# A delta-rule encoder step: faded queries and keys made in the projection stage and kept in DRAM, decay rows from one transposition

## Chip, core and metric

One NeuronCore of a Trainium2 chip. The metric is the device time of one execution in microseconds (us), lower is better. All data are float32; most matrix products are made of three passes with a value split into a rounded high part and a rest.

## What is computed

The reference is one inference step of a two-layer encoder for 2048 prompt tokens and 32 sample tokens with a model width of 1024. Only its first layer is touched here, the gated delta rule with 8 heads of 128:

```
qkv = silu(causal_conv(x @ w_in))          # q, k, v, 4 taps
q = l2norm(q) * 128**-0.5 ; k = l2norm(k)
gcum = cumsum of the log decay within a block of tokens
qdec = q * exp(gcum) ; kdec = k * exp(gcum_last - gcum)
v_new = u - (T (beta k exp(gcum))) S        # what the state recalls for a key
o = qdec S + (q k^T * decay) v_new
S = S * exp(gcum_last) + kdec^T v_new
```

The factor exp(gcum) on queries and keys is called the fade here. Behind the layer stand an output projection with a layer norm, then a sliding-window attention layer; neither is changed.

## The kernel before

**Layout.** Tokens lie along the free axis in the first stage: 2080 columns, in 5 blocks of 416 (TB). In the delta stage they are cut into 17 chunks: 16 of 128 prompt tokens, and one of the 32 sample tokens. Between the two stages q, k, v and the gate z go through DRAM scratch, stored as (chunk, channel, head, token).

**First stage (P1).** 24 rows of 128 output channels (8 heads of q, of k, of v), then 8 of the gate. For each row i:

- `block` (L300), five times: 24 matmuls of 416 columns into one PSUM bank (`project`, L75 to L83), then ScalarE (ACT) copies the bank into the row's buffer R (L305). `ps` (L145) deals the banks out in turn, two from one pool (L108) and four from another (L112); R has two buffers.
- `conv` (L198) for the row just finished, while TensorE (PE) makes the next: ACT writes y = R times the first tap (L206); VectorE (DVE) adds three taps (L209); ACT makes tanh into th (L213); DVE makes silu (L215); SyncE (SP) stores y to q, k or v (L218; the piece of the 32 sample tokens at L220, on ACT's queue before row 15). For q and k ACT squares y into th (L223), DVE transposes th into R (L225) and reduces it to parts (L226). th has one buffer, and in rows 6 to 14 the splitting of the output weights (L1091, `split_out_weights`) borrows it.
- `norms` (L456) after the eighth row of q and of k.

`gates` (L373) is called after rows 0 and 1. It computes the decays and ends in a loop of 17 turns (L422 to L430): PE transposes an 8-column slice of gcum for one chunk, DVE copies it to g_row (one buffer), ACT makes its exponential, and ACT's queue stores both, to `gcum` and `grow` in DRAM.

**What sets the order.** Up to row 15 a scheduler orders each engine's queue. From row 16 on `ordered` (L232) writes the order out by hand for all five engines: each turn of its loop starts row i on PE and `conv(i - 1)`, and between the five blocks advances `conv` (2, 2, 1, 1, 0 steps) and `decays` (L262), which loads `gcum` rows broadcast to all partitions, adds a mask (DVE, L284), makes exponentials (ACT, L288) and stores the decay matrices E (SP, L289; the next load is L277). A weight fetch (L48) is issued in the third block. Engines work their queues in order, so an instruction that waits holds up all that stand behind it on its engine.

**Delta stage (Delta, L605).** `ORDER` is a list of steps with a chunk offset each; for PE, DVE and ACT it is the order of the queues, SP is left to the scheduler. Steps that matter here: `Lk`, `Lq`, `Lgb` load k, q and the decay row of a chunk (`grow`, broadcast to 128 partitions); `G` (L695) are the products of keys; `tk` turns k (L809); `gq` (L822) multiplies queries and keys; `fk`, `fq0`, `fq1` are the fades, products on DVE in place (L832): k after `tk`, q after `gq`; `ks` (L837) recalls with the faded k; `os` (L861) reads the state with the faded q. `L`, `T1` to `T3` and `SPR1` are the transposition and the chain on DVE and GpSimd (POOL) that invert a triangular matrix and end in tcp (L746), which PE needs for y1p (L765). Up to chunk turn 11 the matmuls of the gate rows left over (`GA`) are placed between; after it, not. The output projection of finished chunks is put in at the end.

## Time and profile before

| | |
|---|---|
| median of 3 runs | 2135.41 us (2134.36 to 2135.69) |
| the profiled execution | 2134.49 us, of which its span is 2132.4 us |
| granted clock of PE | 0.996 |
| DMA | 307.25 MB, mean 144 GB/s |

The profile is of one execution. A row of the time line gives start, duration, engine, line of the kernel, operation, output<-inputs, shapes, how many instructions were merged, and in brackets the idle time before it and what ended it. SPq and ACTq are the queues that issue DMAs. In waits, the three numbers are us in total, times, and the longest. Busy time of PE is a modelled time, since matmuls are pipelined.

### The profile page before, as it was taken

The numbers are of one execution on the slowest core, as the hardware profiler recorded it, in microseconds if no ns is written. First come the engines' busy times: TensorE is split into PE (matmuls) and PEld (weight loads), VectorE is DVE, ScalarE is ACT, GpSimd is POOL, SyncE is SP. The second block draws the span as 40 slices with busy tenths as digits, with TensorE's granted clock in tenths as the row PEclk, the third lists the DMA queues.
The fourth block names the chain that finished last, engine by engine and source line by source line (L and its number), as shares of the span: only waits on it lengthen the run. The fifth ranks groups of instructions, "written<-read, shape, count | busy, mean of one in ns | idle before, by whom it ended". The sixth has DMA issues, their size and how long they took to land.

```text
span 2132.4 us, 37157 instructions
## 1 busy us (share of the span) xinstructions
PE 2098.1 (98%) x14062; PEld 1933.3 (91%) x14062; DVE 1305.4 (61%) x2449; ACT 894.0 (42%) x2215; POOL 830.3 (39%) x1179
## 2 busy tenths in 40 slices
PE   8999999999999999999999999999999998999998
PEld 6999999999999999999988888999999996777775
DVE  3676676666557688778977886224543223566665
ACT  4444434446522466667752212312111234455552
POOL 1422222222222277777840201236443113466665
PEclk9999999999999999999999999999999999999999
DMA  5222333256674544446856764556221257534321
GB/s 204 70 62 88 104 110 103 83 145 191 195 215 143 175 158 161 159 150 201 267 178 201 225 211 121 158 174 221 77 78 69 78 132 250 154 99 115 104 71 65
DMA packets 263634, 307.25 MB, mean 144 GB/s; under 512 B 71408, under 2 KB 194608, under 8 KB 263184
## 3 DMA queue, kind: packets, MB, share of 16 engines
q1 hardware_dynamic: 252208, 281.40, 42.3%
q10 hardware_dynamic: 11248, 23.48, 3.4%
q8 instruction: 111, 1.82, 0.4%
q14 instruction: 67, 0.55, 0.1%
HBM read 188.58 MB, written 116.60 MB: 143 GB/s over the span
## 4 chain that ended last, share of the span: by engine, by line
PE 92%; DVE 3%; DMA 3%; ACT 1%; issue 1%; POOL 0%; SPq 0%; ACTq 0%; POOLq 0%; DVEq 0%
PE ps L79 17%; PE ps L81 17%; PE ps L80 17%; PE po L1139 3%; PE ot L1137 3%; PE po L1137 3%; PE po L1138 3%; PE ot L1139 3%; PE ot L1138 3%; PE S L1689 2%; PE ot L1722 2%; PE tr L1704 2%; PE g L695 2%; PE ks L837 1%; PE gq L822 1%; PE op L861 1%
## 5 line engine op out<-in xcount | busy, mean ns | idle before, releaser
L79 PE MATMUL ps<-act_hi,w_hi 128*128 128x416 f32 x1936 | 683.1, 354 | 0.4 <-ACT w_hi L55 0.4
L81 PE MATMUL ps<-act_hi,w_lo 128*128 128x416 f32 x1936 | 681.3, 352 | 1.2 <-POOL w_lo L56 1.2
L80 PE MATMUL ps<-act_lo,w_hi 128*128 128x416 f32 x1936 | 678.1, 350 | 0.4 <-DVE act_lo L71 0.4
L79 PEld LDWEIGHTS ps<-act_hi,w_hi 128*128 128x128 f32 x1936 | 364.1, 188 | 5.5 <-ACT w_hi L55 0.8
L80 PEld LDWEIGHTS ps<-act_lo,w_hi 128*128 128x128 f32 x1936 | 363.7, 188 | 4.8 <-DVE act_lo L71 0.8
L81 PEld LDWEIGHTS ps<-act_hi,w_lo 128*128 128x128 f32 x1936 | 363.4, 188 | 5.0 <-POOL w_lo L56 1.7
L56 POOL TENSOR_TENSOR w_lo<-w_raw,w_hi 128x1024 fp32r<-128x1024 f32 x44 | 117.0, 2658 | 471.6 <-ACT w_hi L55 435.7
L209 DVE SCALAR_TENSOR_TENSOR y<-R,convw,y 128x2083 f32<-128x2083 f32 x72 | 183.0, 2543 | 62.7 <-ACT y L206 47.0
L1528 POOL TENSOR_TENSOR P<-e,sm 128x384 f32<-128x384 f32 (+2 forms) x128 | 101.2, 813 | 182.0 <-DVE sm L1518 176.0
L729 POOL TENSOR_TENSOR tm<-L,Tt 128x60 f32<-128x60 f32 (+19 forms) x365 | 126.1, 345 | 98.1 <-issue 40.0
L731 POOL TENSOR_TENSOR Tt<-Tt,tm 128x60 f32<-128x60 f32 (+19 forms) x365 | 143.4, 393 | 28.6
L1514 ACT ACTIVATE e<-S,nm 128x193 f32<-128x193 f32 (+2 forms) x260 | 104.8, 416 | 95.7 <-DVE nm L1509 58.1
L1137 PE MATMUL ot<-wo,g_hi 128*128 128x512 f32 x256 | 104.6, 409 | 6.2 <-DMA wo<-s_wob 6.2
L305 ACT COPY R<-ps 128x416 f32<-128x416 f32 (+1 forms) x144 | 60.3, 442 | 108.3 <-PE ps L81 95.6
L1137 PE MATMUL po<-wo_hi,g_hi 128*128 128x512 f32 x256 | 103.4, 404 | 0.0
L1336 POOL TENSOR_TENSOR rs<-rs,sin 128x416 f32<-128x416 f32 x50 | 70.7, 1414 | 79.2 <-DVE rs L1335 73.1
L1139 PE MATMUL ot<-wo,g_lo 128*128 128x512 f32 x256 | 101.2, 395 | 0.0
L1138 PE MATMUL ot<-wo,g_hi 128*128 128x512 f32 x256 | 101.1, 395 | 0.0
L1139 PE MATMUL po<-wo_hi,g_lo 128*128 128x512 f32 x256 | 100.2, 391 | 0.5 <-DVE g_lo L1180 0.5
L1138 PE MATMUL po<-wo_lo,g_hi 128*128 128x512 f32 x256 | 99.9, 390 | 0.0
L1421 DVE SCALAR_TENSOR_TENSOR za<-zs,za 128x416 f32<-128x416 f32 x40 | 31.7, 797 | 111.0 <-ACT za L1420 110.6
L55 ACT CAST w_hi<-w_raw 128x1024 fp32r<-128x1024 f32 x46 | 48.4, 1052 | 92.2 <-PE ps L80 73.7
(299 smaller groups left out, 3950.3 us busy)
## 6 DMA issues: line engine op xcount, KB each, us to landing
w_raw<-in_w_in SPq DMA_DIRECT2D x40, 512.0 KB
w_raw<-in_b_w_in SPq DMA_DIRECT2D x18, 512.0 KB
k<-s_k SPq DMA_DIRECT2D x17, 512.0 KB
E<-s_E SPq DMA_DIRECT2D x17, 512.0 KB
s_bz<-za SPq DMA_DIRECT2D x40, 208.0 KB
s_bq<-ra SPq DMA_DIRECT2D x40, 208.0 KB
s_q<-y SPq DMA_DIRECT2D x8, 1024.0 KB
s_wo<-wo_parts SPq DMA_DIRECT2D x16, 512.0 KB
```

The source lines that it names most:

```text
L56: sub.tensor_tensor(out=lo[:], in0=raw[:], in1=hi[:], op=ALU.subtract)
L79: nc.tensor.matmul(ps, hi[:, k, :], xh[:, k, :], start=(k == 0), stop=False)
L80: nc.tensor.matmul(ps, hi[:, k, :], xl[:, k, :], start=False, stop=False)
L81: nc.tensor.matmul(ps, lo[:, k, :], xh[:, k, :], start=False, stop=(k == KC - 1))
L209: nc.vector.scalar_tensor_tensor(out=y[:], in0=R[:, j:j + W], scalar=self.convw[:, i, j:j + 1], in1=y[:], op0=ALU.mult, op1=ALU.add)
L729: P.tensor_tensor(out=tm[:n, i0 - k:, :w], in0=L[:n, i0:, j:j + 1].to_broadcast(sh), in1=Tt[:n, j:j + 1, :w].to_broadcast(sh), op=ALU.mult)
L731: P.tensor_tensor(out=Tt[:n, i0:, :w], in0=Tt[:n, i0:, :w], in1=tm[:n, i0 - k:, :w], op=ALU.subtract)
L1137: nc.tensor.matmul(ps[:n], ghi[:, k, :n], hi, start=a, stop=False)
L1138: nc.tensor.matmul(ps[:n], ghi[:, k, :n], lo, start=False, stop=False)
L1139: nc.tensor.matmul(ps[:n], glo[:, k, :n], hi, start=False, stop=z)
L1514: self.nc.scalar.activation(x.e[:, h, u, :x.n], x.S[:, h, u, :], AF.Exp, bias=x.nm[:, h, u:u + 1], scale=1.0, accum_out=x.sm[:, h, u:u + 1])
L1528: self.nc.gpsimd.tensor_tensor(out=x.P[:, u, :nj * 128].rearrange("r (j h k) -> r j h k", h=2, k=64), in0=x.e[:, :, u, :n].rearrange("r h ...
```

## The change

- **Faded q and k in the first stage.** In rows 2 to 15, after the third tap, SP loads the head's decay row from `grow` into R, broadcast to 128 partitions (`decay_row`). After the squares DVE multiplies y by it into R (`fade`), and SP stores R to new scratch tensors `qf` (rows 2 to 7) or `kf` (rows 8 to 15). The transposition for the norms now goes to y and not to R. The norms of q move from row 7 into row 8.
- **Heads 0 and 1 of q** pass before the decays exist. `fade_again` loads their q back from DRAM into a y buffer and the decay row into th, at the end of the turns i = 19 and 21 of `ordered`, and multiplies and stores them at the start of turns 20 and 22.
- **Delta stage.** The steps `fk`, `fq0`, `fq1` and the load `Lgb` go; `Lkf`, `Lqf0`, `Lqf1` load kf and qf (kf in the one buffer that gb had). q has two half buffers and qf two, where q had five. `ks` reads kf, `os` reads qf. The rest of ORDER keeps its sequence.
- **Decay rows.** Two transpositions in place of 17: one of the sample chunk's 8 columns, one of all 128 columns of the other chunks. Each is copied to g_row, and its exponential made and stored as before.

```diff
@@ -208,6 +208,8 @@
             yield
             nc.vector.scalar_tensor_tensor(out=y[:], in0=R[:, j:j + W], scalar=self.convw[:, i, j:j + 1], in1=y[:],
                                            op0=ALU.mult, op1=ALU.add)
+        if 2 <= i < 16:
+            self.decay_row(h, R)
         yield
         th = one.tile([128, NT + 3], F32, tag="th", name="th")
         nc.scalar.activation(th[:], y[:], AF.Tanh, scale=0.5)
@@ -222,21 +224,58 @@
             return
         nc.scalar.activation(th[:, 0:NP], y[:, 0:NP], AF.Square)
         nc.scalar.activation(th[:, NP:NT], y[:, NP + 3:NP + 3 + NS], AF.Square)
-        nc.vector.transpose(R[:, 0:NT], th[:, 0:NT])
-        nc.vector.tensor_reduce(out=parts[:, h, :], in_=R[:, 0:NT].rearrange("p (c j) -> p c j", j=32),
+        if i == 8:
+            norms(nc, self.G, parts, self.sel, 0, one, self.pt)
+        sq = R
+        if i >= 2:
+            self.fade(kind, h, R, y, R)
+            sq = y
+        nc.vector.transpose(sq[:, 0:NT], th[:, 0:NT])
+        nc.vector.tensor_reduce(out=parts[:, h, :], in_=sq[:, 0:NT].rearrange("p (c j) -> p c j", j=32),
                                 axis=AX.X, op=ALU.add)
         yield
-        if h == 7:
-            norms(nc, self.G, parts, self.sel, kind, one, self.pt)
+        if i == 15:
+            norms(nc, self.G, parts, self.sel, 1, one, self.pt)
+
+    PIECES = (slice(NP + 3, NP + 3 + NS), slice(0, NP))
+
+    def decay_row(self, h, g):
+
+        nc, src = self.nc, self.T["grow"]
+        nc.sync.dma_start(g[:, self.PIECES[0]], src[NTT - 1, h, 0:NS].partition_broadcast(128))
+        nc.sync.dma_start(g[:, 0:NP].rearrange("p (t k) -> p t k", k=128),
+                          src[0:NTT - 1, h, :].partition_broadcast(128))
+
+    def fade(self, kind, h, g, y, out):
+
+        nc, dst = self.nc, self.T[("qf", "kf")[kind]]
+        for s in self.PIECES:
+            nc.vector.tensor_tensor(out=out[:, s], in0=y[:, s], in1=g[:, s], op=ALU.mult)
+        nc.sync.dma_start(dst[NTT - 1, :, h, 0:NS], out[:, self.PIECES[0]])
+        nc.sync.dma_start(dst[0:NTT - 1, :, h, :].rearrange("t p k -> p t k"),
+                          out[:, 0:NP].rearrange("p (t k) -> p t k", k=128))
+
+    def fade_again(self, h):
+
+        q = self.big.tile([128, NT + 3], F32, tag="y", name="y")
+        g = self.one.tile([128, NT + 3], F32, tag="th", name="gb")
+        src = self.T["q"]
+        self.nc.sync.dma_start(q[:, self.PIECES[0]], src[NTT - 1, :, h, 0:NS])
+        self.nc.sync.dma_start(q[:, 0:NP].rearrange("p (t k) -> p t k", k=128),
+                               src[0:NTT - 1, :, h, :].rearrange("t p k -> p t k"))
+        self.decay_row(h, g)
+        yield
+        self.fade(0, h, g, q, q)
 
     def ordered(self, R, parts):
 
         nc, I = self.nc, self.I
         w = split_weights(nc, self.wp, I["w_in"][self.FREE + 1], nc.gpsimd)
         raw = fetch_weights(nc, self.wp, I["w_in"][self.FREE + 2])
-        matrices = None
+        matrices, again = None, iter(())
         for i in range(self.FREE + 1, 24):
             c = self.conv(i - 1, R, parts)
+            drain(again)
             nxt = self.row(i)
             following = split_fetched(nc, self.wp, raw, nc.gpsimd)
             next(c)
@@ -252,6 +291,9 @@
                     matrices = self.decays()
                     next(matrices)
                 self.block(nxt, w, b)
+            if i in (self.FREE + 4, self.FREE + 6):
+                again = self.fade_again((i - self.FREE - 4) // 2)
+                next(again)
             last = c
             R, w = nxt, following
         self.room = self.one, ("parts", "gtmp")
@@ -419,15 +461,15 @@
     nc.scalar.activation(G["ekd"][:, 0:NTT - 1, :], gl[:, 0:NTT - 1, :], AF.Exp)
     nc.scalar.activation(G["ekd"][:32, NTT - 1, :], gl[:32, NTT - 1, :], AF.Exp)
     V.tensor_scalar(out=G["ngc"][:], in0=gc, scalar1=-1.0, scalar2=None, op0=ALU.mult)
-    for t in range(NTT):
-        n = min(128, NT - t * 128)
+    for a, z, n in ((n0, n0 + H, NS), (0, n0, 128)):
+        m = z - a
         tp = pt.tile([128, 512], F32, tag="tp", name="tp")
-        nc.tensor.transpose(tp[:H, :n], gc[:n, t, :], G["ident"][:n, :n])
-        row = one.tile([H, 2, 128], F32, tag="g_row", name="g_row", bufs=1)
-        V.tensor_copy(row[:, 0, :n], tp[:H, :n])
-        nc.scalar.activation(row[:, 1, :n], tp[:H, :n], AF.Exp)
-        nc.scalar.dma_start(T["gcum"][t, :, :n], row[:, 0, :n])
-        nc.scalar.dma_start(T["grow"][t, :, :n], row[:, 1, :n])
+        nc.tensor.transpose(tp[:m, :n], gcf[:n, a:z], G["ident"][:n, :n])
+        row = one.tile([128, 2, 128], F32, tag="g_row", name="g_row", bufs=1)
+        V.tensor_copy(row[:m, 0, :n], tp[:m, :n])
+        nc.scalar.activation(row[:m, 1, :n], tp[:m, :n], AF.Exp)
+        for c, name in enumerate(("gcum", "grow")):
+            nc.scalar.dma_start(T[name].rearrange("t h k -> (t h) k")[a:z, :n], row[:m, c, :n])
 
 
 def add_log(nc, out, x, one, n, w):
...
@@ -656,14 +697,13 @@
         nc, T, n, ti = self.nc, self.T, ch.n, ch.ti
         own = ch.pool is not None and name not in "zE"
         w = n if own else 128
-        if name in ("gb", "k"):
+        if name in ("kf", "k"):
             if own:
                 t = ch.pool.tile([128, 8, w], F32, tag="c" + name, name=name, bufs=1)
             else:
-                t = self.four.tile([128, 8, w], F32, tag=name, name=name, bufs=1 if name == "gb" else self.BUFS)
+                t = self.four.tile([128, 8, w], F32, tag=name, name=name, bufs=1 if name == "kf" else self.BUFS)
             ch.__dict__[name] = t
-            src = T["grow"][ti, :, :n].partition_broadcast(128) if name == "gb" else T["k"][ti, :, :, :n]
-            nc.sync.dma_start(t[:, :, :n], src)
+            nc.sync.dma_start(t[:, :, :n], T[name][ti, :, :, :n])
         elif name == "E":
             ch.E = self.two.tile([128, 8, 128], F32, tag="E", name="E")
             nc.sync.dma_start(ch.E[:n, :, :n], T["E"][ti, :n, :, :n])
@@ -671,8 +711,8 @@
             for q in halves:
                 if own:
                     t = ch.pool.tile([128, 4, w], F32, tag=f"c{name}{q}", name=name, bufs=1)[:]
-                elif name == "q":
-                    t = self.four.tile([128, 4, w], F32, tag="q", name="q", bufs=5)[:]
+                elif name in ("q", "qf"):
+                    t = self.four.tile([128, 4, w], F32, tag=name, name=name, bufs=2)[:]
                 else:
                     t = self.sml.tile([128, 4, w], F32, tag="vz", name=name, bufs=3)[:]
                 ch.__dict__.setdefault(name, {})[q] = t
@@ -827,10 +867,6 @@
         self.nc.vector.tensor_tensor(out=at[:n, :, :n], in0=g[:n, :, :n], in1=ch.E[:n, self.heads(q), :n], op=ALU.mult)
         ch.__dict__.setdefault("at", {})[q] = at
 
-    def fade(self, ch, x, hs):
-        x = x[:, :, :ch.n]
-        self.nc.vector.tensor_tensor(out=x, in0=x, in1=ch.gb[:, hs, :ch.n], op=ALU.mult)
-
     def products(self, ch, pool, name, q, lhs, rhs, n):
         ps = self.bank(pool, ch, f"{name}{q}")
         for j in range(4):
@@ -838,7 +874,7 @@
 
     def recall(self, ch, q):
         n, S = ch.n, ch.S[q]
-        self.products(ch, self.pc, "ks", q, lambda j: ch.k[:, q * 4 + j, :n], lambda j: S[:, j, :], n)
+        self.products(ch, self.pc, "ks", q, lambda j: ch.kf[:, q * 4 + j, :n], lambda j: S[:, j, :], n)
 
     def errors(self, ch, q):
         n, ks, vn = ch.n, ch.__dict__.pop(f"ks{q}"), ch.vn[q]
@@ -858,7 +894,7 @@
         n = ch.n
         op = self.bank(self.pd, ch, f"op{q}")
         for j in range(4):
-            self.nc.tensor.matmul(op[:n, j, :], ch.q[q][:, j, :n], ch.S[q][:, j, :], start=(j == 0), stop=False,
+            self.nc.tensor.matmul(op[:n, j, :], ch.qf[q][:, j, :n], ch.S[q][:, j, :], start=(j == 0), stop=False,
                                   skip_group_check=True)
 
     def seen_inside(self, ch, q):
...
@@ -942,13 +978,12 @@
                    "z": self.gated, "st": self.store}
             for name, f in two.items():
                 S[f"{name}{q}"] = lambda c, f=f, q=q: f(c, q)
-            for name in "qvz":
+            for name in ("q", "qf", "v", "z"):
                 S[f"L{name}{q}"] = lambda c, name=name, q=q: self.load(c, name, (q,))
             S[f"tk{q}"] = lambda c, q=q: self.turn(c, c.k[:, self.heads(q)], f"ktr{q}")
             S[f"tv{q}"] = lambda c, q=q: self.turn(c, c.v[q], f"vtr{q}")
             S[f"kd{q}"] = lambda c, q=q: self.scaled(c, q, "ktr", "kd", "ekd")
             S[f"vn{q}"] = lambda c, q=q: self.scaled(c, q, "vtr", "vn", "hn")
-            S[f"fq{q}"] = lambda c, q=q: self.fade(c, c.q[q], self.heads(q))
         return S
 
     def save(self, ch):
...
@@ -1046,7 +1081,7 @@
             tmp.k = own.k
             tmps.append(tmp)
         yield
-        for name in ("gb", "q", "v"):
+        for name in ("kf", "q", "qf", "v"):
             self.load(chunks[0], name)
         for ch, tmp in zip(chunks, tmps):
             self.load(tmp, "E")
@@ -2162,6 +2197,8 @@
     "q": (NTT, 128, 8, 128),
     "k": (NTT, 128, 8, 128),
     "v": (NTT, 128, 8, 128),
+    "qf": (NTT, 128, 8, 128),
+    "kf": (NTT, 128, 8, 128),
     "z": (NTT, 128, 8, 128),
     "wo": (2, KC, 128, D),
     "wob": (2, KC, 128, D),
```

19 lines of the change are left out of this document (9 added, 10 removed).

## The prediction

> **What bounds the kernel now.** I read the page first: the busy times, then the stretches of time in which an engine could matter, then what TensorE waited for.
>
> ```profile
> PE 2098.1 (98%) x14062; PEld 1933.3 (91%) x14062; DVE 1305.4 (61%) x2449; ACT 894.0 (42%) x2215; POOL 830.3 (39%) x1179
> ```
>
> TensorE (PE) is busy for 2098.1 of 2132.4 us. The change takes work from VectorE (DVE), which is busy 61%, so it can win only where PE waits for DVE. The view of stretches says where that is; its columns are the stretch, its length, then busy time with instruction counts of PE, PEld, DVE, ACT and POOL, the clock, the DMA share and GB/s.
>
> ```profile
> 491.30:513.80 22.50, 22.50 (x121) 22.35 (x121) 13.51 (x10) 13.89 (x33) 5.28 (x5) 1.00 0.65 210
> 829.35:854.51 25.16, 25.16 (x274) 24.20 (x272) 20.95 (x50) 16.98 (x52) 17.55 (x49) 1.00 0.48 157
> 1000.61:1022.16 21.55, 20.75 (x250) 19.80 (x248) 20.66 (x54) 15.22 (x50) 16.81 (x43) 1.00 0.86 281
> 1022.16:1043.69 21.53, 20.49 (x250) 19.84 (x249) 19.58 (x52) 15.81 (x52) 17.66 (x47) 1.00 0.82 275
> 1043.69:1064.64 20.95, 20.39 (x248) 19.78 (x249) 18.68 (x51) 14.62 (x49) 16.37 (x46) 1.00 0.78 266
> 1064.64:1085.50 20.86, 20.09 (x236) 19.10 (x234) 18.32 (x51) 15.21 (x47) 16.98 (x47) 1.00 0.72 233
> ```
>
> The first row is one row of 120 matmuls in the projection stage, 22.50 us, PE never idle. The second is one chunk of the delta stage with the gate's matmuls between: PE never idle either, and DVE at 20.95 of 25.16 costs nothing. The last four are the chunks after the gates are done: here PE idles 0.80, 1.04, 0.56 and 0.77 us, 3.17 us together, while DVE is at 88 to 96%. The list of PE's waits between 990 and 1130 us (total, times, longest) names the cause:
>
> ```profile
> PE y1p L765 <- DVE tcp L746: 2.0, 4, 0.8
> ...
> PE g L695 <- DMA k<-s_k: 0.6, 1, 0.6
> ```
>
> **The change, part by part.**
>
> *Delta stage.* Per chunk it removes three DVE products, whose mean times stand behind the bar:
>
> ```profile
> L832 DVE TENSOR_TENSOR q<-q,gb 128x512 f32<-128x512 f32 (+1 forms) x34 | 25.7, 760 | 0.0
> L832 DVE TENSOR_TENSOR k<-k,gb 128x1024 f32<-128x1024 f32 (+1 forms) x17 | 20.3, 1195 | 13.3 <-PE ktr L809 13.3
> ```
>
> That is 2 x 0.76 + 1.20 = 2.7 us of DVE per chunk, 46 us in all. Before 1000 us PE hides it. After that, the product on k stands just ahead of the transposition and the chain that end in tcp, so the four waits for tcp (2.0 us) should go. A k tile is last read by the turn to ktr and the pairs, no longer by the recall, so its buffer is free earlier and the wait for k (0.6 us) should go too: **-2.6 us**. Bounds: -3.2 (all idle time of the four stretches) and 0, since the stage gets 512 KB more to load per chunk (qf; kf takes gb's place) where the DMA share is already 0.72 to 0.86. I take nearly the whole because qf and kf have about a chunk of time to land.
>
> *Decay rows.* 15 of 17 transpositions go. What one costs PE is seen from the starts around it:
>
> ```profile
> 138.43 0.34 PE L80 MATMUL ps<-act_lo,w_hi 128*128 128x416 f32 x1
> 138.61 0.27 PE L425 MATMUL tp<-ident,gtmp 128*8 128x128 f32 x1
> 138.64 0.44 PE L81 MATMUL ps<-act_hi,w_lo 128*128 128x416 f32 x1
> 138.91 0.35 PE L79 MATMUL ps<-act_hi,w_hi 128*128 128x416 f32 x1
> ```
>
> Two projection matmuls take 0.48 us around it; at 22.50 us for 120 they take 0.38. So 0.10 us each, 15 of them **-1.5 us**.
>
> *The projection rows 2 to 15.* Each gets a 1 MB load of the decay row into R, a product over 2080 columns (2 x 1.20 = 2.4, with the short piece 2.5 us of DVE) and a 1 MB store out of R. The transposition now writes y and so waits until y's own store has landed. One row of before on DVE:
>
> ```profile
> 266.94 8.19 DVE L209 SCALAR_TENSOR_TENSOR y<-R,convw,y 128x2083 f32<-128x2083 f32 x3 [4.78 <-ACT y L206]
> 277.19 2.33 DVE L215 SCALAR_TENSOR_TENSOR y<-th,y 128x2083 f32<-128x2083 f32 x1 [2.06 <-ACT th L213]
> 282.12 2.35 DVE L225 STREAM_TRANSPOSE R<-th 128x2080 f32<-128x2080 f32 x1 [2.60 <-ACT th L224]
> 284.50 2.32 DVE L226 TENSOR_REDUCE parts<-R 128x65 f32<-128x2080 f32 x1
> 289.11 8.29 DVE L209 SCALAR_TENSOR_TENSOR y<-R,convw,y 128x2083 f32<-128x2083 f32 x3 [2.29 <-ACT y L206]
> ```
>
> The price of a 1 MB transfer in 512-byte pieces comes from y's store and the traffic behind it (same columns as above):
>
> ```profile
> 279.54 0.38 SPq L218 DMA_DIRECT2D s_k<-y  x1
> ```
>
> ```profile
> 268.00:269.00 1.00, 1.00 (x7) 1.00 (x6) 1.00 (x1) 0.10 (x1) 0.09 (x1) 1.00 0.94 381
> 280.00:284.00 4.00, 4.00 (x23) 3.96 (x22) 1.88 (x1) 2.41 (x3) 0.00 (x0) 1.00 0.80 247
> 284.00:285.00 1.00, 1.00 (x7) 0.99 (x6) 0.97 (x2) 0.00 (x0) 0.00 (x0) 1.00 0.25 76
> ```
>
> 4 x 247 + 76 = 1064 KB end about 284.6: 5.1 us from issue to end, of which some 3.7 us are traffic. So: decay row issued at 275.1, landed 280.3; product 280.3 to 282.8; y's store landed about 284.7; transposition and reduction until 289.4 instead of 286.8, and the next row starts 0.3 us late. DVE then has 22.5 us per row against PE's 22.50. The new store (issued 282.8, behind y's) lands about 288.6; the row after next first writes R here:
>
> ```profile
> 290.19 0.51 ACT L305 COPY R<-ps 128x416 f32<-128x416 f32 x1 [0.61 <-PE ps L81]
> ```
>
> So I cost these rows at **0**. What covers them is tight in time but deep: a row's blocks go through six PSUM banks (two of L108, four of L112), so PE can run 6 x 4.5 = 27 us from a block's start before that block's copy must be done. SP gets five more issues per row; its weight fetch waits for POOL as before. If the cover fails, see the third rival.
>
> *The first of these rows.* The decay rows must lie in DRAM before row 2 can load them.
>
> ```profile
> 124.14 0.56 ACT L305 COPY R<-ps 128x384 f32<-128x384 f32 x2
> ```
>
> ```profile
> 134.39 0.31 ACTq L430 DMA_DIRECT2D s_grow<-g_row  x1
> 136.34 1.47 ACT L305 COPY R<-ps 128x416 f32<-128x416 f32 x3 [2.01 <-DVE parts L226]
> ```
>
> The second g_row store goes out at 134.4 and lands about 136.3 (an estimate: 5.1 less 3.7 us of traffic); the load of row 2 lands at 141.4, its product ends at 145 behind row 3's work, its store ends at 150 to 152 behind row 3's load and store. R is copied into then, not at 136.3. Row 4 starts at about 123 (row 3's last copy is at 124.1), so its first bank is wanted back at 150. PE stands 0 to 2.5 us; I take **+1**.
>
> *Heads 0 and 1 again.* Their rows pass before the decays exist, so fade_again loads q and the decay row (2 MB) at the end of the 19th and 21st turn, and its products stand at the head of DVE's queue in the next turn. That order is written out by hand, for DVE, ACT and SP too. Behind the products wait, on DVE, the first E addition and all products of the convolution; behind these, on ACT, the exponentials and the copies that free PE's banks; on SP, behind the stores, the E transfers and the weight fetch.
>
> ```profile
> 496.73 3.24 SPq L220 DMA_DIRECT2D s_v<-y  x1
> 500.08 0.50 SPq L289 DMA_DIRECT2D s_E<-E  x1
> 500.68 0.39 SPq L277 DMA_DIRECT2D E<-s_gcum  x1
> ```
>
> ```profile
> 496.55 0.69 DVE L284 TENSOR_TENSOR E<-E,nm 128x512 f32<-128x512 f32 x1 [1.85 <-ACT R L305]
> 499.43 5.13 DVE L209 SCALAR_TENSOR_TENSOR y<-R,convw,y 128x2083 f32<-128x2083 f32 x2 [2.19 <-ACT y L206]
> ```
>
> SP comes to the loads at 501.1 (in turn 19 it is already late: the short store behind a 1 MB one takes 3.24 us). The short piece takes 0.4, then 5.1 + 3.7 us for two transfers: landed 510.3; product 2.5; E addition 0.7. The convolution starts at 513.5 and not 499.4: 14.1 us late, twice. Little is regained between:
>
> ```profile
> 509.34 0.48 ACT L305 COPY R<-ps 128x416 f32<-128x416 f32 x1
> ...
> 551.19 0.48 ACT L305 COPY R<-ps 128x416 f32<-128x416 f32 x1
> ...
> 558.74 0.57 ACT L305 COPY R<-ps 128x384 f32<-128x384 f32 x2 [1.60 <-PE ps L81]
> ```
>
> The copies of second blocks in turns 20 and 22 lie 41.85 us apart, 20.9 per row against PE's 22.5: the chain already runs as fast as it can there. Row 22 ends on PE at 558.7, so row 23's third block, which needs the bank of row 22's second, starts at 567.7; its copy ends at 551.7, 16.0 us to spare. After: 2 x 14.1 - 2 (for a wait of ACT on weights that may go) = 26.2 us late, and PE stands 26.2 - 16.0 = **+10.2 us**. In turn 20 alone the same sum leaves about 1 us (510 + 14 against 522.7), which is part of it. Bounds: 0 if the lateness of the two stays under 16 us, 14 without the regained part and with slower loads.
>
> *The norms of q* only move by a row. *Sum* against the profiled execution's own 2134.49 us: -2.6 - 1.5 + 0 + 1 + 10.2 = +7.1, so 2141.6. The runs' median, 2135.41, lies 0.9 higher: **2142.5 us**, 0.33% slower.
>
> **The rivals.**
>
> 1. *fade_again is hidden, and the change is faster.* PE needs nothing from DVE directly; banks alone tie it. If DVE is late by 8 us per turn or less, PE never stands: 2135.41 - 2.6 - 1.5 + 0 to 1 = 2131.3 to 2132.3; with the full 3.2 us, 2130.7. For it: in turn 17 of before DVE does 12 us of norms and PE shows no wait. Against it: there are two, and 2 MB cannot land in 8 us by the store's row. It decides whether the load plus product end before 507 us. Chance 0.25, half of it below 0.2%.
> 2. *Loads are faster than stores.* The row at 268 us shows 381 GB/s for loads: 2 MB in 5.5 us instead of 7.4, lateness 12.2 each, 24.4 - 2 - 16.0 = +6.4, so 2138.7. Chance 0.13. The Trainium skill ("DMA: Bandwidth & Descriptors", "Anatomy of one DMA") fits 2.0 us plus bytes over 436 GB/s, for DMAs issued from GpSimd; by that, 2 MB take an estimated 6.8 us, close to this rival. No load of 1 MB in such pieces is in the trace.
> 3. *Rows 2 to 15 get late.* If y's store lands 2 us later than reckoned, DVE needs 24.5 us per row, and 12 rows lose 24 us, which the banks no longer cover (about 18 us); what is left adds to the stall of fade_again: 2150 to 2165. For it: 22.5 against 22.50. Against: DVE's order here is the scheduler's, which can fill the wait with the next row. Chance 0.10.
> 4. *Faster than reckoned*, by a wait that I don't see: below 2130. Chance 0.04.
>
> **How the numbers follow.** The forecast has 0.48: its own range is 2139.8 to 2149. 0.2%, about what a measurement can tell from no change, is 4.3 us: faster is below 2131.1, slower above 2139.7. Slower: 0.48 + 0.10 = 0.58. Faster: half of the first rival and the fourth, 0.13 + 0.04 = 0.17. Same: the rest, 0.25. The range 2130.5 to 2150 leaves out most of rival 3 and rival 4 and the edges of the others.
>
> **What would show it.** Of the changed profile: PE without the four waits for tcp near 1000 to 1085 us; 2 transpositions at L425's place; a PE wait of 0 to 2.5 us near 150 us for an ACT copy; waits of the products in fade for DMA of some 10 us near 500 and 550 us, and a PE wait for an ACT copy of R, together about 10 us, between 520 and 580. If PE shows no wait there, rival 1 is right and my bank arithmetic or the transfer's price is wrong. If DVE shows long waits of the transposition for y's store in every row and PE waits before 400 us, it is rival 3.

## The result and the profile after

The changed kernel takes **2304.49 us** (median of 4 runs, 2303.67 to 2305.59); the kernel before, run beside it, 2135.55 (2134.36 to 2136.03). The ratio is **1.0792, 95% interval 1.0779 to 1.0805**: 7.9% slower. The forecast was 2142.5, with a range to 2150; the sign was right, the size not.

The page of the changed kernel, its busy times and, of the 40 slices, those of PE, of its granted clock and of DMA:

```profile
PE 2122.9 (92%) x14047; PEld 1952.8 (85%) x14047; DVE 1307.8 (57%) x2415; ACT 887.2 (39%) x2200; POOL 794.3 (34%) x1179
...
PE   8979678873986999999999999999999999899998
...
PEclk9989889986998999999999999999999999999999
DMA  5244445443666666555588467454621217734331
```

Everything is lost in the first 13 slices (some 58 us each), the rows of the projection stage. The span is 2303.8 us, so PE idles 2303.8 - 2122.9 = 180.9 us, and before 2132.4 - 2098.1 = 34.3: **146.6 us more idle**. PE is also 24.8 us longer busy (2122.9 - 2098.1) with 15 instructions fewer. Together that is the 171.4 us by which the span grew (2303.8 - 2132.4). DMA, at 0.4 to 0.5, is not full in these slices.

PE's waits (total, times, longest), and DVE's:

```profile
PE ps L79 <- ACT R L347: 83.7, 11, 16.5
PE n_ps L504 <- DVE parts L234: 51.4, 2, 27.6
PE ps L81 <- POOL w_lo L56: 12.3, 2, 11.0
...
PE g L735 <- DMA k<-s_k: 1.1, 1, 1.1
```

```profile
DVE R L253 <- DMA R<-s_grow: 156.7, 14, 15.5
...
DVE y L253 <- DMA gb<-s_grow: 56.2, 4, 16.2
```

The waits for tcp are gone, as forecast, and the one for k near 1040 us too (the 1.1 us shown here stand at the start of the delta stage). But the product that fades a row (L253) waits for the decay row in each of the 14 rows, 11.2 us on the mean. The transfers, in KB and us from issue to landing, say why:

```profile
R<-s_grow SPq DMA_DIRECT2D x14, 1024.0 KB, 15.7
...
s_q<-y SPq DMA_DIRECT2D x8, 1024.0 KB, 11.7
s_k<-y SPq DMA_DIRECT2D x8, 1024.0 KB, 15.0
s_kf<-R SPq DMA_DIRECT2D x8, 1024.0 KB, 5.1
```

The store of the faded row takes 5.1 us, just what the prediction took for 1 MB. The load of the decay row takes 15.7, and y's store, issued behind it, is held up with it. One row on SP and on DVE:

```profile
277.74 0.43 SPq L246 DMA_DIRECT2D R<-s_grow  x1
282.38 0.37 SPq L220 DMA_DIRECT2D s_q<-y  x1
282.85 11.96 SPq L254 DMA_DIRECT2D s_qf<-R  x1
```

```profile
261.68 2.29 DVE L253 TENSOR_TENSOR R<-y,R 128x2048 f32<-128x2048 f32 x1 [11.48 <-DMA R<-s_grow]
...
294.81 2.29 DVE L253 TENSOR_TENSOR R<-y,R 128x2048 f32<-128x2048 f32 x1 [12.23 <-DMA R<-s_grow]
298.00 2.35 DVE L233 STREAM_TRANSPOSE y<-th 128x2080 f32<-128x2080 f32 x1 [0.89 <-DMA s_q<-y]
```

From the load's issue to the product go 294.81 - 277.74 = 17.1 us. Only then y's store lands and the transposition starts. SP's queue stands 11.96 us at the second issue behind the load, until 294.81, when the load has landed. A row takes 294.81 - 261.68 = 33.1 us on DVE, where PE needs 22.5. PE feels it through R: the late product makes the store out of R late, ACT can't copy a block into R before that store has landed, and PE's bank isn't free before the copy:

```profile
270.29 0.51 ACT L347 COPY R<-ps 128x416 f32<-128x416 f32 x1 [14.35 <-DMA s_qf<-R]
270.85 0.72 PE L79 MATMUL ps<-act_hi,w_hi 128*128 128x416 f32 x1 [10.51 <-ACT R L347]
```

Two stretches of that row, while the load runs and when the stores move, then a longer one (columns as in the prediction):

```profile
284.00:294.00 10.00, 0.00 (x0) 0.00 (x0) 0.00 (x0) 4.28 (x6) 2.61 (x3) 0.54 0.21 67
296.00:300.00 4.00, 0.00 (x0) 0.00 (x0) 3.11 (x2) 0.00 (x0) 0.00 (x0) 0.50 0.93 278
250.00:300.00 50.00, 20.55 (x98) 19.25 (x96) 21.73 (x11) 15.21 (x18) 8.25 (x9) 0.75 0.46 143
```

While the load runs, with y's store already issued behind it, 67 GB/s are moved at a DMA share of 0.21; when the stores move, 278 at 0.93. The load is slow without being limited by the DMA engines' time. PE stands in both, and its granted clock is down to 0.50. It is still low when PE goes on:

```profile
304.89 2.19 PE L504 MATMUL n_ps<-parts,sel 128*128 128x136 f32 x8 [23.83 <-DVE parts L234]
...
307.58 0.55 PE L80 MATMUL ps<-act_lo,w_hi 128*128 128x416 f32 x1
307.93 0.55 PE L81 MATMUL ps<-act_hi,w_lo 128*128 128x416 f32 x1
...
309.02 0.35 PE L79 MATMUL ps<-act_hi,w_hi 128*128 128x416 f32 x1
309.20 0.35 PE L80 MATMUL ps<-act_lo,w_hi 128*128 128x416 f32 x1
```

At 307.6 the matmuls start 0.35 us apart, at 309.0 0.18. Such stretches behind the stalls are where PE is longer busy.

### The profile page after: what moved, and what is told of

It is laid out like the page before. It is cut to its first block, busy times and chain, and to the rows that moved or that the text cites. A ratio compares the mean times of both kernels' runs of the same rounds, so it can differ in the third digit from the quotient of the medians.

```text
span 2303.8 us, 37254 instructions
## 1 busy us (share of the span) xinstructions
PE 2122.9 (92%) x14047; PEld 1952.8 (85%) x14047; DVE 1307.8 (57%) x2415; ACT 887.2 (39%) x2200; POOL 794.3 (34%) x1179
## 4 chain that ended last, share of the span: by engine, by line
PE 62%; DMA 14%; DVE 11%; SPq 3%; issue 2%; ACT 2%; POOL 0%; ACTq 0%; DVEq 0%; POOLq 0%
PE ps L79 7%; PE ps L81 7%; PE ps L80 7%; DMA s_k<-y 5%; DVE y L209 5%; PE po L1174 3%; PE ot L1172 3%; PE po L1172 3%; PE po L1173 3%; PE ot L1174 2%; PE ot L1173 2%; PE S L1724 2%; DMA s_q<-y 2%; PE ot L1757 2%; PE tr L1739 2%
## 5 line engine op out<-in xcount | busy, mean ns | idle before, releaser
L79 PE MATMUL ps<-act_hi,w_hi 128*128 128x416 f32 x1936 | 694.7, 360 | 86.8 <-ACT R L347 83.7
L81 PE MATMUL ps<-act_hi,w_lo 128*128 128x416 f32 x1936 | 690.2, 357 | 12.3 <-POOL w_lo L56 12.3
L80 PE MATMUL ps<-act_lo,w_hi 128*128 128x416 f32 x1936 | 687.3, 355 | 0.4 <-DVE act_lo L71 0.4
L79 PEld LDWEIGHTS ps<-act_hi,w_hi 128*128 128x128 f32 x1936 | 371.6, 192 | 96.4 <-ACT R L347 88.0
L81 PEld LDWEIGHTS ps<-act_hi,w_lo 128*128 128x128 f32 x1936 | 370.4, 191 | 16.9 <-POOL w_lo L56 13.4
L80 PEld LDWEIGHTS ps<-act_lo,w_hi 128*128 128x128 f32 x1936 | 371.0, 192 | 5.3 <-DVE act_lo L71 0.8
L769 POOL TENSOR_TENSOR tm<-L,Tt 128x60 f32<-128x60 f32 (+19 forms) x365 | 117.8, 323 | 114.7 <-DVE tm L769 46.2
L771 POOL TENSOR_TENSOR Tt<-Tt,tm 128x60 f32<-128x60 f32 (+19 forms) x365 | 131.8, 361 | 28.6
L253 DVE TENSOR_TENSOR R<-y,R 128x32 f32<-128x32 f32 (+1 forms) x28 | 34.8, 1242 | 157.1 <-DMA R<-s_grow 156.7
## 6 DMA issues: line engine op xcount, KB each, us to landing
R<-s_grow SPq DMA_DIRECT2D x14, 1024.0 KB, 15.7
```

What stands on the lines that cost most here:

```text
L79: nc.tensor.matmul(ps, hi[:, k, :], xh[:, k, :], start=(k == 0), stop=False)
L80: nc.tensor.matmul(ps, hi[:, k, :], xl[:, k, :], start=False, stop=False)
L81: nc.tensor.matmul(ps, lo[:, k, :], xh[:, k, :], start=False, stop=(k == KC - 1))
L769: P.tensor_tensor(out=tm[:n, i0 - k:, :w], in0=L[:n, i0:, j:j + 1].to_broadcast(sh), in1=Tt[:n, j:j + 1, :w].to_broadcast(sh), op=ALU.mult)
L771: P.tensor_tensor(out=Tt[:n, i0:, :w], in0=Tt[:n, i0:, :w], in1=tm[:n, i0 - k:, :w], op=ALU.subtract)
```

## The experiments

Three questions: what makes the load slow (e1, e2, e8, e10, e12, e15, e16); what the parts of the change are worth by themselves (e3, e4); and what keeps the whole change above the kernel before once the load is mended (e5 to e7, e9, e11, e13, e14). The theories of the first question changed on the way: A, B and C are in e1's expectation, P in e15's.

### The load

**e1_contig** stores the decay rows head by head, so that a partition reads one run of 8 KB and not 16 pieces of 512 bytes.

```diff
-        nc.sync.dma_start(g[:, 0:NP].rearrange("p (t k) -> p t k", k=128),
-                          src[0:NTT - 1, h, :].partition_broadcast(128))
+        nc.sync.dma_start(g[:, 0:NP], self.T["rows"][h, :].partition_broadcast(128))
```

The rows come from a third transposition, of a copy of gcum in the order (head, chunk).

> The changed kernel, with the decay rows stored a second way, (head, token), so that the broadcast load of a head's row reads 8 KB in one run per partition instead of 16 pieces of 512 bytes; one more transposition makes that layout. Theory A (the broadcast in 512-byte pieces is what is slow): the load lands in about 5 us instead of 15.7, y's store no longer waits behind it, the PE waits before 800 us go, and the time is 2130 to 2145 us; what is left over 2132 is the stall of fade_again. Theory B (128 partitions that read the same 8 KB of DRAM are slow whatever the pieces): the load still takes about 15 us and the time stays near 2300 us. Theory C (any 1 MB load in 512-byte pieces is slow): fast here too, as in A; the run with distinct pieces tells A from C.

Measured: 2154.47 us (4 runs; before on this chip 2133.98), ratio 1.0093 (1.0080 to 1.0107). Its transfers, then PE's waits, then three stretches:

```profile
R<-s_rows SPq DMA_DIRECT2D x14, 1024.0 KB, 5.8
...
s_k<-y SPq DMA_DIRECT2D x8, 1024.0 KB, 5.3
```

```profile
PE ps L79 <- ACT R L346: 11.0, 3, 6.9
PE n_ps L512 <- DVE parts L234: 7.3, 1, 7.3
```

```profile
100.00:400.00 300.00, 300.00 (x1595) 297.21 (x1594) 233.65 (x128) 128.42 (x165) 69.41 (x75) 1.00 0.60 185
400.00:450.00 50.00, 42.72 (x220) 42.00 (x219) 41.48 (x46) 14.97 (x18) 10.06 (x12) 0.93 0.38 114
550.00:600.00 50.00, 40.91 (x201) 39.66 (x200) 21.50 (x18) 24.98 (x54) 7.35 (x9) 0.90 0.74 220
```

The same 1 MB lands in 5.8 us, y's store in 5.3, and PE is busy in all of 100 to 400 us. 150 of the 169 us were the load's form (2304.5 - 2154.5 of 2304.5 - 2135.5). What is left sits in two places, 400 to 450 and 500 to 600 us.

**e2_distinct** keeps the 512-byte pieces but reads other data in every partition (q of head 0).

```diff
-                          src[0:NTT - 1, h, :].partition_broadcast(128))
+                          self.T["q"][0:NTT - 1, :, 0, :].rearrange("t p k -> p t k"))
```

> The changed kernel, but the 1 MB load into R takes the 512-byte pieces of head 0's q, a different address for every partition, instead of the decay row, so the faded q and k are wrong. Same size, same pieces, same place, no broadcast. Theory A (broadcast in small pieces): it lands in 5 to 8 us and the time is 2130 to 2160 us, with fade_again's two slow loads left. Theory C (any load in 512-byte pieces): it lands in about 15 us and the time stays near 2300 us. Theory B (same addresses): fast, as in A.

Measured: 2157.61 us (one run), landing:

```profile
R<-s_q SPq DMA_DIRECT2D x14, 1024.0 KB, 6.3
```

So neither small pieces by themselves nor a read by all partitions alike (e1) is slow. For the latter there is a second case: the delta stage of before loads the same rows for all 128 partitions in runs of 4 KB, and in e3_rows_only these 512 KB land in 4.7 us. Two things to keep in mind of e2: its pieces also lie at other distances than those of after, and its second fade uses the same load, so that, other than its expectation says, no slow load is left in it.

**e8_pieces1k** reads 1 KB pieces 8 KB apart: `src[0:NTT - 1:2, m:m + 2, :]` for `src[0:NTT - 1, h, :]`.

> The kernel after with the 1 MB decay-row load cut into 1 KB pieces instead of 512-byte ones, still read by all 128 partitions alike and still 8 KB apart (each piece holds a chunk of two neighbouring heads, so half of the values are another head's decay and the fade is wrong). If the price of the load is per piece, the landing falls from 15.7 to about 8 us, near the 5.8 us of 8 KB runs, and the time to about that of e1_contig, 2155 to 2175. If it is the reading of one place by 128 partitions from far places, whatever the piece, it stays at 13 to 16 us and the time above 2250.

Measured: 2293.57 us (one run).

```profile
R<-s_grow SPq DMA_DIRECT2D x14, 1024.0 KB, 14.8
```

Half as many pieces gain hardly anything, so the price is not simply one per piece. The test is not a clean one: the pieces of after lie 4 KB apart, not 8 as the expectation has it, so e8 doubles the distance too.

**e10_halves** cuts e1_contig's load in two, every other chunk in each: 512-byte pieces 1 KB apart.

```diff
+        for a in range(2):
+            nc.sync.dma_start(g[:, 0:NP].rearrange("p (b a k) -> p a b k", a=2, k=128)[:, a],
+                              src[h, :].rearrange("(b a k) -> a b k", a=2, k=128)[a].partition_broadcast(128))
```

> The kernel of e1_contig with the load of a decay row of 8 KB cut into two DMAs, one for every other chunk: 512-byte pieces again, read alike by 128 partitions, but 1 KB apart within one 8 KB row instead of 4 KB apart over 64 KB. If pieces of 512 bytes read alike by all partitions are slow wherever they lie (as after's 15.7 us for 1 MB), the two take 14 to 16 us together, and the time is 2250 or more. If it is how far apart the pieces lie, they land as in e1_contig, 6 to 8 us after their issue, and the time is 2150 to 2165.

Measured: 2194.77 us (one run), between the two answers. One row, SP's issue and DVE's product:

```profile
263.88 4.94 SPq L247 DMA_DIRECT2D R<-s_rows  x2
```

```profile
273.02 3.85 DVE L254 TENSOR_TENSOR R<-y,R 128x2048 f32<-128x2048 f32 x1 [4.39 <-DMA R<-s_rows]
```

273.02 - 263.88 = 9.1 us for 1 MB, where after needs 17.1. But the halves don't run side by side. In the waits of SP's queue L247 waits 14 times for R<-s_rows, 49.7 us in all: SP issues the second half only when the first has landed. Each half lands quickly:

```profile
R<-s_rows SPq DMA_DIRECT2D x28, 512.0 KB, 4.2
```

So 512-byte pieces read alike are not slow when they lie 1 KB apart, as the second answer has it; the 9.1 us are two such loads, one after the other. (The product takes 3.85 us here instead of 2.29; why is open.)

**e12_copies** stores `grow` twice; each half of the partitions reads its own copy.

> The kernel after with the decay rows stored twice, and each half of the partitions reading its own copy in a DMA of its own (512-byte pieces 4 KB apart as in after, each place read by 64 partitions instead of 128). If the load is slow because 128 readers want the same place at the same time, two copies halve the crowd: R<-s_grow and R<-s_grow2 land in 8 to 10 us and the time falls to 2160 to 2220. If each such DMA is slow by its form (how a broadcast of far pieces is cut into descriptors), the two take about as long together, 14 to 16 us, and the time stays at 2290 to 2310.

Measured: 2270.12 us (one run).

```profile
R<-s_grow SPq DMA_DIRECT2D x28, 512.0 KB, 11.4
```

```profile
264.50 1.30 SPq L247 DMA_DIRECT2D R<-s_grow  x2
```

```profile
278.86 2.29 DVE L254 TENSOR_TENSOR R<-y,R 128x2048 f32<-128x2048 f32 x1 [9.59 <-DMA R<-s_grow]
```

14.4 us for both: half as many readers of a place, in two DMAs, help by 2.7 us, no more.

**e15_pitch6k** and **e16_pitch4k5** change only the distance of the pieces: scratch `grow` gets rows of 192 or 144 numbers, of which 128 are used.

```diff
-    "grow": (NTT, 8, 128),
+    "grow": (NTT, 8, 144),
...
-                          src[0:NTT - 1, h, :].partition_broadcast(128))
+                          src[0:NTT - 1, h, 0:128].partition_broadcast(128))
```

> The kernel after with its decay rows of 512 bytes stored 768 bytes apart, so that the 16 pieces of one head lie 6 KB apart instead of 4 KB; every piece is still 512 bytes and read alike by 128 partitions. Theory P (the distance of 4 KB, a power of two, makes all 16 pieces meet at one place of the memory): the landing falls from 15.7 us towards the 6 us of the kernels with long runs or with pieces that differ, and the time to 2155 to 2200. Theory B (128 readers that want the same 512 bytes one after the other, wherever the next piece lies): it stays at 14 to 16 us and 2290 to 2310.

> The same with 576 bytes from row to row, so 4.5 KB between the pieces of one head. By theory P the pieces fall on different places too: 6 to 9 us and 2155 to 2230. By theory B nothing changes: 14 to 16 us, 2290 to 2310; a part of the rows now starts off a 256-byte border, which may add to it.

Measured: 2203.52 and **2153.62 us** (one run each). The landings of the first and of the second:

```profile
R<-s_grow SPq DMA_DIRECT2D x14, 1024.0 KB, 9.4
```

```profile
R<-s_grow SPq DMA_DIRECT2D x14, 1024.0 KB, 6.5
```

e16 comes out as theory P says: 64 bytes of padding per 512-byte row, nothing else, take the load from 15.7 to 6.5 us and 151 us off the kernel. e15 does so only in part, with 9.4 us and a time just above the 2155 to 2200 that it was given. Theory B, which had 14 to 16 us for both, is out. Put together, for 1 MB to 128 partitions:

| kernel | piece | apart | read alike | us to land | time, us |
|---|---|---|---|---|---|
| after | 512 B | 4 KB | by all | 15.7 | 2304.5 |
| e8 | 1 KB | 8 KB | by all | 14.8 | 2293.6 |
| e12 | 512 B | 4 KB | by 64, two copies | 14.4 (both) | 2270.1 |
| e15 | 512 B | 6 KB | by all | 9.4 | 2203.5 |
| e10 | 512 B | 1 KB | by all | 4.2 for each half; 9.1 for both, one after the other | 2194.8 |
| e16 | 512 B | 4.5 KB | by all | 6.5 | 2153.6 |
| e2 | 512 B | 512 KB | no (4 KB from partition to partition) | 6.3 | 2157.6 |
| e1 | 8 KB | one run | by all | 5.8 | 2154.5 |

(14.4 and 9.1 run from the issue to the product; on that count after has 17.1.)

### The parts alone

**e3_rows_only** is the kernel before with the two transpositions of after in place of 17, nothing else.

> The kernel before, with only the decay rows by two transpositions instead of 17. By the prediction's term 15 x 0.10 us = 1.5 us less, 2134.0 us. Rival: nothing (2135.5), if the shift of other work gives the time back.

Measured: 2137.46 us (11 runs) against 2133.98, ratio 1.0015 (1.0006 to 1.0025), 3.5 us slower. No gain shows; why it is slower the waits of PE don't settle. The loss doesn't add up with other parts either: e11 and e14 below hold these two transpositions and a third, and are as fast as e4, which has the old 17.

**e4_delta_only** is the kernel before with the delta stage of after, where kf and qf are loaded from the unfaded k and q.

> The kernel before with only the delta stage of the change: no fades on DVE, and a load of q and k a second time in the place of qf and kf, so the fade is left out of the result. By the prediction's term 2.6 us less (2132.9 us), the four waits for tcp gone. Rival: the added 512 KB per chunk make loads late and give it back (2135 to 2140).

Measured: 2130.20 us (11 runs), ratio 0.9980 (0.9971 to 0.9989), 3.8 us faster. No wait for tcp or for k is left.

### What is left once the load is mended

**e5_late_fade**, **e6_late_norms** and **e7_both** move two places in the order written out by hand, on e1_contig.

```diff
-            drain(again)                     # at the head of the turn
...
                 for j in range((2, 2, 1, 1, 0)[b]):
                     next(c, None)
+                    if b == 1 and j == 0:
+                        drain(again)         # e5, e7
...
-                if i == self.FREE + 2 and b == 1:
+                if i == self.FREE + 2 and b == 3:   # norms of k, e6, e7
```

> The kernel of e1_contig with the products of the second fade (heads 0 and 1 of q) put not at the head of the next turn but behind the three products of the next row's convolution, so that DVE works on those while the two loads land. Theory (the prediction's own term): in e1_contig the 10.2 to 11.0 us of PE waits for ACT's copies of R come from DVE standing still for 2 x 16 us ahead of those products; then DVE's wait for gb falls from 32.1 to under 16 us, the PE waits for R near 531 and 579 us go, and the time falls by 10 to 15 us (the waits, and the granted clock of 0.90 behind them) to 2140 to 2145. Rival: PE waits there because the row's stores and the decay matrices crowd the queues, and DVE's wait is harmless; then the waits for R stay at 8 to 11 us and the time at 2152 to 2157.

> The kernel of e1_contig with the norms of k and the start of the decay matrices put two blocks later in the order written out by hand (two more of the decay matrices' steps are taken in the next two turns). Theory: the 7.3 us wait of n_ps in e1_contig is DVE's lateness at row 15, about one and a half blocks, and it is paid only because PE's order has the norms there; then the wait goes, no other takes its place, and the time falls by 7 to 12 us (wait and clock) to 2142 to 2148. Rival: DVE is late for good behind the rows, so the same 7 us come up at the next thing that PE waits for from DVE or ACT (the copies of R of the next turns), and the time stays within 2152 to 2157.

> Both edits of e5_late_fade and e6_late_norms on the kernel of e1_contig: the whole change, with decay rows stored for long reads and with two places of the order moved. If both theories hold the time is 2154.5 less 11.0 less 7.3 and less the granted clock that those stalls cost (0.4 points of the span, some 8 us by the clocks 0.992 and 0.996): 2126 to 2134, so at or below the kernel before (about 2134), with the delta stage's 3.8 us as the only gain. If either rival holds it stays above 2140.

Measured, before on this chip 2134.11: e5 2143.06, ratio 1.0044 (1.0030 to 1.0057); e6 2163.06, 1.0129 (1.0114 to 1.0143); e7 2143.80, 1.0047 (1.0033 to 1.0061). PE's waits in e5:

```profile
PE n_ps L513 <- DVE parts L234: 6.7, 1, 6.7
```

and in e6:

```profile
PE ps L79 <- ACT R L346: 20.1, 4, 10.3
```

In e5 the waits for R are gone and 11 us with them: the products at the head of a turn were their cause. e6 doesn't gain (three of its runs took 2163, the fourth 2155.16): the wait for n_ps goes down to 0.6 us, but the lateness comes up in the turns of the second fade, 20.1 us where e1_contig has 11.0. That was the rival, and worse. With both, 5.4 us of waits for R stay in e7, which is no faster than e5; the two waits are not two separate prices. Its row on ACT:

```profile
510.03 2.04 ACT L206 ACTIVATE y<-R,convw 128x2083 f32<-128x2083 f32 x1 [6.57 <-DMA s_v<-y]
```

The second fade takes one of two y buffers, so the next row's first copy waits 6.57 us for a store.

**e9_pair** takes that wait away: the second fade uses the y buffer that the row before has just left, and its loads and products are moved apart.

```diff
-        y = self.big.tile([128, NT + 3], F32, tag="y", name="y")
+        y = self.big.tile([128, NT + 3], F32, tag=f"y{i % 2}", name="y", bufs=1)
```

> The kernel of e7_both with the second fade's q in the y buffer that the row before has just left: the two y buffers get a name each, the decay row is asked for at the end of a turn, q one block into the next, and the products run two blocks in, ahead of the row's tanh. Theory: in e7_both the second fade takes the y buffer that the next row's first copy needs, so that copy waits 6.57 us for the store of v before it, DVE's first product comes 8.96 us late, and ACT, with its order fixed, copies R late; then the PE waits for R (5.4 us in e7_both) fall under 1 us and the clock between 500 and 575 us, 0.96 and 0.90 in two windows, goes to 1.00: about 8 to 10 us less, 2133 to 2137. Rival: the second fade's 6 MB of loads and stores are too much for that stretch, where DMA is busy 0.7 to 0.88, whatever buffer they use; then E<-s_gcum and the weights come late, the PE waits stay at 4 us or more and the time within 2140 to 2146.

Measured: 2146.04 us (before 2135.22), ratio 1.0054 (1.0041 to 1.0066): no better than e7. Of PE's waits:

```profile
PE g L749 <- DMA k<-s_k: 4.5, 1, 4.5
PE ps L79 <- ACT R L352: 4.4, 4, 1.5
```

The time is the rival's (2140 to 2146): the waits for R spread over four places and the delta stage's first k comes later. That the crowded DMA is the cause, as the rival says, isn't shown. Away from the head of the turn (e5, e7, e9), where exactly the second fade stands matters little.

**e11_no_again_norms** is e6_late_norms without the second fade.

> The kernel of e6_late_norms without the second fade: q of heads 0 and 1 goes to the faded store as it is (the fade of these two heads is left out). What is left of the change then is the delta stage, the faded rows 2 to 15, the two transpositions and one more for the long rows. By the terms so far: before 2134, delta stage -3.8, transpositions +3 (e3_rows_only), rows 2 to 15 nothing: 2131 to 2136, with no PE wait for R between 500 and 600 us. If the rows 2 to 15 themselves cost (their stores and loads, DVE's lateness passed on), it is above 2138 and PE waits for R or n_ps come up before 470 us.

Measured: 2130.91 us (10 runs), ratio 0.9981 (0.9972 to 0.9991). Between 500 and 600 us, where e1_contig loses most, PE never idles:

```profile
500.00:600.00 100.00, 100.00 (x533) 99.36 (x532) 63.62 (x45) 60.21 (x126) 25.02 (x22) 1.00 0.62 191
```

So the 14 faded rows cost nothing here, with the norms of k two blocks later, and the second fade is worth about 13 us in e7_both and 15 in e9_pair. Whether the norms must stand later once the second fade is gone was not tried.

**e13_in_delta** and **e14_in_delta_late** do that work elsewhere: q of heads 0 and 1 is stored unfaded and multiplied in the delta stage, 128 x 256 per chunk.

```diff
+    def fade_two(self, ch):
+        x = ch.qf[0][:, 0:2, :ch.n]
+        self.nc.vector.tensor_tensor(out=x, in0=x, in1=ch.gb[:, :, :ch.n], op=ALU.mult)
...
-        ... Lqf0+1 v5+0 ... PC3+1 vn0+1 ... ks0+1 e0+1 U32+1
+        ... Lqf0+1 Lgb+1 v5+0 ... PC3+1 fq0+1 vn0+1 ... ks0+1 e0+1 U32+1    # e13
+        ... Lqf0+1 Lgb+1 v5+0 ... PC3+1 vn0+1 ... ks0+1 e0+1 fq0+1 U32+1    # e14
```

> The kernel of e11_no_again_norms made whole again: q of heads 0 and 1 is stored unfaded and faded in the delta stage, one product of 128 x 256 for each chunk, with a load of 128 KB of decay rows, in the place that the product of that quad of q had in the kernel before. Theory: the second fade in the first stage is what keeps e7_both 13 us above e11_no_again_norms, and the one small product is off the delta stage's path; then this takes 2131 to 2133.5, below the kernel before (2134 to 2135.5) by 0.1 to 0.2%. Rival: leaving the work out, not moving it, made e11_no_again_norms fast (the delta stage's own gain came from DVE being free of fades at those places), so the waits of y1p for tcp come back (2.0 us before) and with them the time of before or a little more, 2134 to 2137.

> The kernel of e13_in_delta with the product for heads 0 and 1 later in the order of a chunk (behind the errors of the first four heads instead of ahead of the scaled keys of the next chunk but one). In e13_in_delta DVE stood 24.0 us at this product for the load of qf, which is asked for only a few steps ahead of it, and the PE waits for npr (14.3 us, 1000 to 1100 us) came behind that. Theory: the loads have landed by the later place, the waits of DVE for qf fall under 3 us and those of PE for npr go; the small product itself costs nothing: 2130 to 2133.5, below the kernel before. Rival: any more work on DVE in the delta stage is on its path, then the waits of PE for DVE stay at 2 us or more in the stage and the time is 2134 to 2140; and if the load waits for its buffer and not for its time, the 24 us stay and the time is 2150 or more.

Measured: e13 2158.82 us (before 2134.10), ratio 1.0113 (1.0099 to 1.0128). e14 **2129.99 us** (11 runs; before 2134.23), ratio **0.9980 (0.9971 to 0.9989)**. In e13 PE waits for npr, and DVE between 780 and 1120 us for qf:

```profile
PE ktr L867 <- DVE npr L760: 10.5, 5, 4.7
```

```profile
DVE qf L737 <- DMA qf<-s_qf: 24.0, 5, 7.6
```

The stretch of 1000 to 1100 us, in e13 and then in e14:

```profile
1000.00:1100.00 100.00, 87.54 (x979) 84.25 (x978) 69.32 (x197) 59.73 (x195) 61.94 (x182) 0.91 0.72 246
```

```profile
1000.00:1100.00 100.00, 97.75 (x1127) 93.02 (x1126) 80.33 (x228) 69.44 (x227) 66.73 (x194) 1.00 0.88 295
```

The same product, placed a few steps behind its load, makes PE idle 12.5 us of 100; placed later, 2.3. e14 computes all that the reference asks for and beats both kernels, the one before by 0.2%: it has the delta stage's gain, faded rows at no cost, and no second fade in the first stage.

## Why the prediction was wrong, step by step

**Rows 2 to 15, forecast 0: the step that failed.** The prediction priced the decay-row load by y's store ("The price of a 1 MB transfer in 512-byte pieces comes from y's store"), 5.1 us from issue to landing. Size and pieces were the same; the addresses were not. The load, read alike by all 128 partitions in pieces 4 KB apart, takes 15.7 us. That row of before was a store to distinct places, so it could not bound this load from above, and the range had no bound for it. With the load at 5.8 or 6.5 us (e1, e16) these rows cost what was forecast: in e1 PE is busy in all of 100 to 400 us, and e11, which has them all, is faster than before.

Rival 3 named the place and the mechanism (DVE over 22.5 us per row, banks used up), but its price was 2 us per row for y's store; a row measured 33.1 us, 10.6 above PE's. The sign that it named, a long wait of the transposition for y's store, did not come either: that wait is 0.89 us, the one of the product for the load 12.23. From the same line of the forecast follow most of the waits for n_ps (51.4 us) and for w_lo (12.3), DVE's and SP's lateness seen from other places: with the load mended they are 7.3 and 1.2 us (e1). The norms of q, which "only move by a row", stand for 23.8 of the 51.4, and for none in e1.

**The first of these rows, forecast +1.** After has PE standing 15.04 us at 166 us; with the load mended no wait is there (e1).

**The second fade, forecast +10.2: right in size.** With the load mended, PE waits 11.0 us (e1) and 10.5 (e16) for copies of R between 520 and 590 us, and e5 shows that DVE's standing at the head of the turn made them. That the sum came this near is in part luck: DVE stands 36.3 us at these products in e1 (32.1 for the short piece and 4.2 for the long one), where the forecast had it late by 2 x 14.1. In after, where the same slow load feeds these fades too, DVE waits 56.2 us there and PE most of all here:

```profile
730.92 0.72 PE L79 MATMUL ps<-act_hi,w_hi 128*128 128x416 f32 x1 [16.47 <-ACT R L347]
```

The whole price, against e11, is some 13 to 15 us even in the better places of e7 and e9. The waits listed for PE don't cover all of it, so what else it consists of stays open.

**Missed: the norms of k.** DVE is about 10 us late at row 15, and the hand-written order asks PE for the norms there: 7.3 us in e1. The prediction saw that DVE needed 22.5 of 22.5 us per row and let the banks cover the rest ("PE needs nothing from DVE directly"), but these matmuls read DVE's result, and no bank helps. As a sum, 2142.5 + 7.3 is 2149.8, near e1's 2154.5; but e6 and e7 show that the wait can't be taken off by itself.

**Delta stage, forecast -2.6.** Measured alone -3.8 (e4; by its interval -2.3 to -6.2), so right within the error.

**Transpositions, forecast -1.5.** Measured alone +3.5 (e3; +1.3 to +5.3): wrong in sign. Why stays open; in e11 and e14 no such loss shows.

**What stays open.** The runs show that the distance of the pieces decides: read alike by all partitions, 512 bytes 4 KB apart are slow, 6 KB apart half mended, 4.5 KB apart and 1 KB apart fast. A power of two is not the mark by itself, since 1 KB is fast and 6 KB is not. That the common reading is needed too is likely from e2 and e12 but not shown, since e2 changes the distances as well. What unit behind the addresses the readers crowd at is not seen. The Trainium skill ("DMA: Bandwidth & Descriptors", "Latency and other measured facts") reports about half the rate for row pitches of 4 and 8 MiB, and full rate with 4 KiB of padding, and infers, unverified, that streams in lock-step meet on one memory channel. This case points the same way, with 512 bytes more on a distance of 4 KB; whether it is the same effect no run here shows.

## What to carry to other kernels

A transfer's price depends on where its reads fall, not only on its bytes and the size of its pieces: look for a row with the same addresses before using its duration, and if there is none, bound the cost from a bad case. Where many partitions read the same strided pieces, store them as one run, or try another distance and read the landing time. Work that must be done late, outside the loop that hides it, is better moved to the place that has its data anyway, and at enough steps behind its load.

## What the hardware showed unexpectedly

- A broadcast of 512-byte pieces 4 KB apart ran at 67 GB/s, with the DMA engines busy 0.21 of the time; 64 more bytes per row made 1 MB land in 6.5 instead of 15.7 us.
- A load of this kind holds up what is queued behind it: y's store landed in 15.0 instead of 5.3 us (s_k of after and of e1), and SP stood 11.96 us at an issue.
- PE's granted clock is 0.50 to 0.54 in stretches where it stands, and it is not back at once: after the stall that ends at 304.89 the matmuls start 0.35 us apart up to 308.6, and 0.18 to 0.19 us apart from 308.8 on. In sum PE was 24.8 us longer busy. The Trainium skill ("TensorE: Matmul & The Clock Gate", "Part 1: The HAM clock gate") gives half rate after an idle window of about 3.4 us. With PE idle from 281.1 (304.89 - 23.83), the 0.54 of 284 to 294 and the 0.50 of 296 to 300 agree.
